# DeltaNet inverse in a hybrid decoder trunk: the first doubling on two quarters of the array, and sums of squares by a column of ones

## The chip, the core and the metric

The kernel runs on one core of one Trainium2 chip. The metric is the device time of one execution in microseconds. The core's engines work side by side: TensorE (PE, matmul; PEld is its weight load), VectorE (DVE), ScalarE (ACT), GpSimd (POOL) and SyncE (SP, which only issues loads and stores here). They wait for each other by semaphores. Matrix products go to PSUM, in banks of 128 partitions by 512 numbers of four bytes.

## The reference

A decoder trunk of two layers over 256 tokens of width 2048, batch 1. Each layer normalises its input, multiplies it by one wide input matrix, mixes the result in two ways, maps it back by one output matrix and adds a gated per-layer embedding. Half of the mixing width is a gated DeltaNet with 8 heads of 128, in chunks of tokens:

```python
q = l2_norm(to_heads(q, DN_HEADS)) * (DN_HEAD_DIM ** -0.5)
k = l2_norm(to_heads(k, DN_HEADS))
...
A = jnp.where(strict, jnp.einsum("bhncd,bhnsd->bhncs", k_beta, k) * decay, 0.0)
eye = jnp.eye(C, dtype=A.dtype)
rhs = jnp.concatenate([v * beta[..., None], k_beta * jnp.exp(G)[..., None]], axis=-1)
sol = lax.linalg.triangular_solve(A + eye, rhs, left_side=True, lower=True,
                                  unit_diagonal=True)
```

Two things matter here. `l2_norm` needs, for each token and head, the sum of the squares of q and of k. And the solve needs the inverse of a unit triangular matrix. The kernel takes chunks of 128 tokens, so it inverts a 128x128 matrix for each head and each of two chunks. The other half of the mixing width is HGRN2, which the change leaves as it is.

## The kernel before

**The big products.** All weights come through `load` as tiles of 128 x 1024 (SyncE's queue, three raw buffers). `prep` splits each into a rounded part (ScalarE, L333) and the rest (VectorE, L335). `products` makes three matmuls for each weight tile from the split weights and activations, mostly 512 columns wide. `run_step` handles one such tile: 24 matmuls for two halves of the tokens. `ahead` keeps the splits two steps and the loads four steps ahead. All these, and all other matmuls, go through `PEOrder` (L274 to L281), which keeps TensorE in the order in which the program writes them. L276 is therefore the line of every matmul and L279 that of every transpose.

**The order of the rest.** A layer runs the stages "in", "out" and "gate". While their big products run, the mixers' small work is put between them: each mixer is a set of Python generators, which `spawn` starts and `tick`, called after each big step, goes on with. A `yield n` means "go on after n steps". The n of every stop are written out by hand in `DELAY` by kind (d is DeltaNet, h is HGRN2), with exceptions by group and stop in `DELAY_AT` (L32 to L48); `wait` reads them. A generator can also wait for a flag with `after`. There are four groups g of two heads in each of two layers, so eight DeltaNet units `DN`, named dn00 to dn13 in the profile (layer, group).

**One DeltaNet unit.** `dkdq` turns k and q, runs the convolution and leaves both in `kq`, tokens along the free side, for two heads hh and two chunks t. `k_side` calls `stat(0, "ssk")`: four transposes into PSUM, then four squares on ScalarE that also add up along the row. The transposed k is used again for `ktail`. From the sums come `invn` and `b`. `q_side` forms the products of k with k and q (pg), and from them `Bt` and `QK`; it sends `Bt` through DRAM on ScalarE's queue to get the 16x16 diagonal blocks F together; then comes `stat(1, "ssq")` for q; then it inverts the diagonal blocks on VectorE (L639 to L644) and brings them back through DRAM as `Tt`.

From there the inverse doubles three times, from blocks of 16 to 32, 64 and 128 (L650 to L703). Each doubling transposes a part of `Tt` (stops t16, t32, t64), makes the product pp with `Bt`, copies it to `Pp` on ScalarE (stops p16, p32, p64), makes the product px with `Tt` and writes it into `Tt`. The first doubling does this with full 128x128 products for each of the four (hh, t) pairs i and puts the result in by a mask (L662). The second works on 32x32 blocks in two parts b = 0 and 64, with all i of one part and then all of the other (L669, L678). The third works on 64x64 blocks. `dv` waits for the inverse and finishes the unit.

**Buffers.** `tmp` takes from a ring of six tiles of 128 x 512 that all mixers share; PSUM has five banks for the mixers (`pm`) and three for the big products (`pd`).

Of the kernel before, what the change touches and what calls it, by code (L numbers as in the profile page):

```python
# [25 lines left out]
def chunk_cols(chunk):  # L26
# [6 lines left out]
    "d": {'c': 1, 'D': 4, 'k': 5, 'q': 5, 'ssq': 1, 'F': 3, 'T': 9, 't16': 2, 'p16': 2, 't32': 2, 'p32': 2, 't64': 2, 'p64': 2, 'v': 5, 'z0': 1, 'S': 1, 'w': 1, 'z1': 1, 'o': 1, 'y': 3, 'yp': 1},  # L33
# [98 lines left out]
UNITS = (1, 4, 16)  # L132


NMASK = 128 + 3 * 192


def const_arrays():
    i = np.arange(128)
    c = np.zeros((128, 4 * 128 + 256), np.float32)  # L140
    c[:, 0:128] = np.eye(128)
    c[:, 128:256] = 1.0
    c[:, 256:384] = i[:, None] > i[None, :]
    c[:, 384:512] = i[:, None] <= i[None, :]
    c[:, 512:768] = (np.arange(256) % 128 != 0)[None, :]
    s, r = i[:, None], i[None, :]
    m = np.zeros((128, NMASK), np.int32)
    m[:, 0:128] = (s // 32 == r // 32) & (s % 32 < 16) & (r % 32 >= 16)
    for n, u in enumerate(UNITS):
        o = 128 + 192 * n  # L150
# [9 lines left out]
def trunk(ctx: ExitStack, tc: tile.TileContext, xT, x, pT, W, par, fw, cst, msk, eye, out):  # L160
# [338 lines left out]
    class DN:  # L499
# [62 lines left out]
        def stat(self, w, name):  # L562

            ps = pm.tile([128, 512], F32, tag="m", name=self.n + name)
            for i in range(4):
                PE.transpose(ps[:, 128 * i:128 * i + 128], self.kq[:, i // 2, i % 2, w, :], ident)
            ss = small(name)
            for i in range(4):
                S.activation(sp.tile([128, 128], F32, tag="junk", name="junk", bufs=1), ps[:, 128 * i:128 * i + 128],
                             AF.Square, accum_out=ss[:, i:i + 1])  # L570
            return ps, ss
# [12 lines left out]
        def k_side(self):  # L584
# [3 lines left out]
            pk, ss = self.stat(0, "ssk")  # L588
            self.ktail = mix("ktail", 256, 1, n + "kt")
            V.tensor_tensor(v4(self.ktail), v4(pk)[:, 0::2], v4(self.Dt)[:, 0::2, 127:128].to_broadcast([128, 2, 128]),  # L590
# [12 lines left out]
        def q_side(self):  # L603
# [7 lines left out]
            for hh in range(2):  # L611
# [4 lines left out]
                for t in range(2):  # L616
# [14 lines left out]
                            channel_multiplier=-1)  # L631
            yield self.wait("ssq")
            pq, ss = self.stat(1, "ssq")
# [18 lines left out]
            yield self.wait("t16")  # L652
            pp = pm.tile([128, 512], F32, tag="m", name=n + "pp16")
            for i in range(4):
                PE.matmul(pp[:, 128 * i:128 * i + 128], Bt[:, i], v4(Tn)[:, i], start=True, stop=True)
            Pp = tmp(n + "P16")
            S.copy(Pp, pp)
# [4 lines left out]
            V.copy_predicated(Tt, bc1(ms[:, 0:128], 4), v4(px))  # L662
# [6 lines left out]
            for b in (0, 64):  # L669
                for i in range(4):  # L670
# [7 lines left out]
            for b in (0, 64):  # L678
                for i in range(4):
# [87 lines left out]
    class HG:  # L767
# [42 lines left out]
        def q_side(self, qr):  # L810
# [38 lines left out]
            def quad_products(u, K, Q):  # L849
                for hh in range(2):  # L850
# [6 lines left out]
                    o, mo = 0, 128 + 192 * UNITS.index(u)  # L857
# [285 lines left out]
```

## Time and profile before

| | |
|---|---|
| median of 3 runs | 1306.22 us (1305.85 to 1307.09) |
| the profiled execution's own time | 1306.57 us |
| its span, first to last instruction | 1304.9 us |
| granted TensorE clock, mean | 0.995 of full speed |
| TensorE busy (matmuls; weight loads) | 1271.2 us; 1066.3 us |
| VectorE, ScalarE, GpSimd busy | 960.6, 780.1, 105.5 us |
| matmul instructions | 6592 |

The span is that of one execution under the profiler. A busy TensorE overlaps its instructions, so the sum of lengths isn't the time that they take. A float32 product appears in the trace as two matmuls with a weight load each.

### The profile page before, as it was taken

To read this page: it belongs to the slowest core of one execution; us is meant where nothing else is said; L and a number is where in the kernel's file an instruction comes from. 1 tells how busy PE (TensorE), PEld (TensorE's weight loads), DVE (VectorE), ACT (ScalarE), POOL (GpSimd) and SP (SyncE) were. 2 spreads that over 40 slices of the span, in tenths; PEclk is the share of its full clock that TensorE was granted. 3 is DMA by queue.
4 is the path that set the end of the run, shared out by engine and by line. 5 is a ranking of instruction groups with operands and counts; after the bars stand their busy time and mean duration, and the time that the engine had idled before them with its cause. 6 is when DMAs were issued, how large, how long until landed. Compare 5 with 4: busy or idle time off the path is not lost.

```text
span 1304.9 us, 18389 instructions
## 1 busy us (share of the span) xinstructions
PE 1271.2 (97%) x6592; PEld 1066.3 (82%) x6592; DVE 960.6 (74%) x1787; ACT 780.1 (60%) x1389; POOL 105.5 (8%) x88
## 2 busy tenths in 40 slices
PE   7999999999999999999999999999999999999995
PEld 6888788888888888888888887888888888888884
DVE  5689877976798766547558897788877968565575
ACT  5766666666665654347557666667656666443464
POOL 0200010010001110000001100111100012000010
PEclk9999999999999999999999999999999999999998
DMA  9555455445554455665555554544555444555553
GB/s 321 187 172 155 146 157 167 132 150 179 156 173 154 130 174 175 192 189 185 187 170 176 153 162 154 172 144 139 161 186 174 138 162 146 187 186 183 193 193 114
DMA packets 78172, 221.01 MB, mean 169 GB/s; under 512 B 15488, under 2 KB 24576, under 8 KB 78080
## 3 DMA queue, kind: packets, MB, share of 16 engines
q1 hardware_dynamic: 59408, 212.49, 51.1%
q10 hardware_dynamic: 18672, 7.34, 2.2%
q8 instruction: 52, 0.85, 0.3%
q14 instruction: 40, 0.33, 0.1%
HBM read 215.08 MB, written 4.72 MB: 168 GB/s over the span
## 4 chain that ended last, share of the span: by engine, by line
PE 69%; DVE 18%; ACT 5%; issue 3%; DMA 3%; POOL 0%; ACTq 0%; SPq 0%; DVEq 0%
PE gate L276 13%; PE out L276 12%; DVE wlo L335 6%; PE in0hf L276 5%; PE in1dk L276 5%; PE in1hf L276 5%; PE in1dv L276 5%; PE in0dv L276 4%; PE in0hi L276 3%; PE in1hi L276 3%; PE in0dk L276 2%; DMA raw<-W 2%; ACT whi L333 2%; PE up L276 2%; PE in1dz L276 1%
## 5 line engine op out<-in xcount | busy, mean ns | idle before, releaser
L335 DVE TENSOR_TENSOR wlo<-raw,whi 128x1024 fp32r<-128x1024 f32 (+2 forms) x398 | 485.5, 1223 | 245.9 <-ACT whi L333 244.3
L333 ACT ACTIVATE whi<-raw 128x1024 fp32r<-128x1024 f32 (+2 forms) x398 | 414.6, 1044 | 342.1 <-PE out L276 84.4
L276 PE MATMUL in0dk<-whi,n0hi 128*128 128x512 f32 x128 | 51.6, 403 | 2.5 <-ACT whi L333 2.5
L276 PE MATMUL in1dk<-whi,n1hi 128*128 128x512 f32 x128 | 51.2, 400 | 2.4 <-ACT pg L981 2.4
L276 PE MATMUL in0dk<-wlo,n0hi 128*128 128x512 f32 x128 | 50.8, 397 | 1.8 <-DVE wlo L335 1.6
L276 PE MATMUL in1hf<-whi,n1hi 128*128 128x512 f32 x128 | 52.0, 406 | 0.0
L276 PE MATMUL in0hf<-whi,n0hi 128*128 128x512 f32 x128 | 52.0, 406 | 0.0
L276 PE MATMUL in0hi<-whi,n0hi 128*128 128x512 f32 x128 | 51.9, 406 | 0.0
L276 PE MATMUL in1hi<-whi,n1hi 128*128 128x512 f32 x128 | 51.9, 406 | 0.0
L276 PE MATMUL in1dk<-wlo,n1hi 128*128 128x512 f32 x128 | 50.1, 391 | 0.9 <-DVE wlo L335 0.8
L276 PE MATMUL in1hi<-wlo,n1hi 128*128 128x512 f32 x128 | 50.1, 391 | 0.5 <-DVE wlo L335 0.5
L276 PE MATMUL in0dk<-whi,n0lo 128*128 128x512 f32 x128 | 50.5, 395 | 0.0
L276 PE MATMUL gate<-whi,g0hi 128*128 128x512 f32 x128 | 50.1, 392 | 0.0
L276 PE MATMUL in0hi<-wlo,n0hi 128*128 128x512 f32 x128 | 50.0, 391 | 0.1
L276 PE MATMUL in1hf<-whi,n1lo 128*128 128x512 f32 x128 | 50.0, 391 | 0.0
L276 PE MATMUL in0hf<-whi,n0lo 128*128 128x512 f32 x128 | 50.0, 391 | 0.0
L276 PE MATMUL in1hi<-whi,n1lo 128*128 128x512 f32 x128 | 50.0, 390 | 0.0
L276 PE MATMUL in0hi<-whi,n0lo 128*128 128x512 f32 x128 | 50.0, 390 | 0.0
L276 PE MATMUL in1dk<-whi,n1lo 128*128 128x512 f32 x128 | 49.9, 390 | 0.0
L276 PE MATMUL in0hf<-wlo,n0hi 128*128 128x512 f32 x128 | 49.9, 390 | 0.0
L276 PE MATMUL in1hf<-wlo,n1hi 128*128 128x512 f32 x128 | 49.9, 390 | 0.0
L276 PE MATMUL gate<-whi,g1hi 128*128 128x512 f32 x128 | 49.9, 390 | 0.0
(1575 smaller groups left out, 3304.8 us busy)
## 6 DMA issues: line engine op xcount, KB each, us to landing
raw<-W SPq DMA_DIRECT2D x384, 512.0 KB, 3.5
raw<-W SPq DMA_DIRECT2D x8, 544.0 KB, 4.4
xt<-xT SPq DMA_DIRECT2D x4, 512.0 KB, 6.3
h<-x SPq DMA_DIRECT2D x4, 512.0 KB, 8.7
out_dram<-h SPq DMA_DIRECT2D x6, 256.0 KB, 3.1
fw<-fw ACTq DMA_DIRECT2D x2, 512.0 KB, 4.9
pin<-pT ACTq DMA_DIRECT2D x2, 256.0 KB, 3.0
out_dram<-h ACTq DMA_DIRECT2D x2, 256.0 KB, 2.8
```

The costliest lines, as they stand in the source:

```text
L276: return tc.keep_in_program_order(nc.tensor.matmul(*a, **k))
L333: S.activation(hi[:, sl], raw[:, sl], AF.Copy)
L335: V.tensor_tensor(lo[:, sl], raw[:, sl], hi[:, sl].bitcast(F32), ALU.subtract)
```

## The change

The statistic's method is replaced by two, `squares` (one square on ScalarE from `kq` into a temporary) and `sums` (four matmuls with the squares as weights and one column of ones, whose result is one column each). k keeps two of its four transposes, those that `ktail` reads, and gets one more step between the square and the sums; q keeps none, and its square is made before the stop ssq.

The first doubling works on two quarters of the array, rows and columns 0 to 63 and 64 to 127, and moves only the 16 columns of each block of 32 that can be other than zero; its copy spreads the result out again, its masked copy becomes two, and the mask shrinks from 128 to 32 columns. The second doubling gets its two loops exchanged, so that the two parts alternate. Beside that the table of delays changes.

```diff
-    "d": {'c': 1, 'D': 4, 'k': 5, 'q': 5, ...
+    "d": {'c': 1, 'D': 4, 'k': 4, 'q': 5, ...
...
-    "d0D": 5, "d0k": 6, "d0p16": 3, "d0q": 6, "d0t64": 3, "d0v": 6,
-    "d1S": 3, "d1p64": 1, "d1ssq": 3, "d1t16": 4, "d1yp": 2,
-    "d2D": 5, "d2k": 4, "d2t64": 4, "d2y": 4, "d2yp": 2, "d2z1": 2,
-    "d3k": 6, "d3o": 2, "d3p64": 3, "d3v": 6,
-    "h0K": 2, "h0a": 4, "h0u16": 3, "h0yp": 2,
-    "h1f": 2, "h1u": 3, "h1x": 3, "h1yp": 3,
+    "d0D": 5, "d0F": 2, "d0k": 7, "d0p16": 4, "d0p64": 1, "d0q": 7, "d0t16": 1, "d0yp": 3,
+    "d1D": 6, "d1S": 3, "d1p64": 1, "d1q": 4, "d1ssq": 3, "d1t16": 4, "d1y": 4, "d1yp": 2, "d1z1": 2,
+    "d2D": 5, "d2k": 5, "d2p32": 1, "d2t32": 1, "d2t64": 4, "d2y": 4, "d2yp": 2, "d2z0": 2, "d2z1": 2,
+    "d3k": 5, "d3o": 2, "d3p64": 3, "d3v": 6,
+    "h0K": 2, "h0a": 4, "h0c": 2, "h0u1": 1, "h0u16": 3, "h0yp": 2,
+    "h1f": 2, "h1u": 3, "h1yp": 3,
...
-    "h3K": 1, "h3f": 2, "h3y": 3, "h3yp": 2,
+    "h3K": 1, "h3f": 2, "h3u1": 3, "h3y": 3, "h3yp": 2,
...
-NMASK = 128 + 3 * 192
+NMASK = 32 + 3 * 192
...
-    m[:, 0:128] = (s // 32 == r // 32) & (s % 32 < 16) & (r % 32 >= 16)
+    m[:, 0:32] = (s % 64 // 32 == np.arange(32)[None, :] // 16) & (s % 32 < 16)
...
-        def stat(self, w, name):
-
-            ps = pm.tile([128, 512], F32, tag="m", name=self.n + name)
-            for i in range(4):
-                PE.transpose(ps[:, 128 * i:128 * i + 128], self.kq[:, i // 2, i % 2, w, :], ident)
-            ss = small(name)
-            for i in range(4):
-                S.activation(sp.tile([128, 128], F32, tag="junk", name="junk", bufs=1), ps[:, 128 * i:128 * i + 128],
-                             AF.Square, accum_out=ss[:, i:i + 1])
-            return ps, ss
+        def squares(self, w, name):
+            sq = tmp(self.n + name)
+            S.activation(sq, self.kq.rearrange("p h t w c -> p (h t) w c")[:, :, w, :], AF.Square)
+            return sq
+
+        def sums(self, ps, o, sq):
+
+            for i in range(4):
+                PE.matmul(ps[:, o + i:o + i + 1], sq[:, 128 * i:128 * i + 128], ones[:, 0:1], start=True, stop=True)
+            return ps[:, o:o + 4]
...
-            pk, ss = self.stat(0, "ssk")
+            sq = self.squares(0, "k2")
+            yield 1
+            pk = pm.tile([128, 512], F32, tag="m", name=n + "ssk")
+            for hh in range(2):
+                PE.transpose(pk[:, 128 * hh:128 * hh + 128], self.kq[:, hh, 0, 0, :], ident)
+            ss = self.sums(pk, 256, sq)
...
+            sq = self.squares(1, "q2")
             yield self.wait("ssq")
-            pq, ss = self.stat(1, "ssq")
+            ss = self.sums(pm.tile([128, 512], F32, tag="m", name=n + "ssq"), 0, sq)
...
             pp = pm.tile([128, 512], F32, tag="m", name=n + "pp16")
-            for i in range(4):
-                PE.matmul(pp[:, 128 * i:128 * i + 128], Bt[:, i], v4(Tn)[:, i], start=True, stop=True)
+            two = lambda ap: ap.rearrange("p (b c) -> p b c", b=2)
+            for i in range(4):
+                for b in (0, 64):
+                    PE.matmul(pp[b:b + 64, 32 * i:32 * i + 32], Bt[b:b + 64, i, b:b + 64],
+                              two(v4(Tn)[b:b + 64, i, b:b + 64])[:, :, 0:16], start=True, stop=True)
             Pp = tmp(n + "P16")
-            S.copy(Pp, pp)
+            S.copy(Pp[:, :256].rearrange("p (a w b) -> p a w b", w=2, b=16),
+                   pp[:, :128].rearrange("p (a b) -> p a b", b=16).unsqueeze(2).to_broadcast([128, 8, 2, 16]))
             yield self.wait("p16")
             px = pm.tile([128, 512], F32, tag="m", name=n + "px16")
             for i in range(4):
-                PE.matmul(px[:, 128 * i:128 * i + 128], v4(Pp)[:, i], Tt[:, i], start=True, stop=True)
-            V.copy_predicated(Tt, bc1(ms[:, 0:128], 4), v4(px))
+                for b in (0, 64):
+                    PE.matmul(px[b:b + 64, 32 * i:32 * i + 32], Pp[b:b + 64, 64 * i:64 * i + 64],
+                              two(Tt[b:b + 64, i, b:b + 64])[:, :, 16:32], start=True, stop=True)
+            for b in (0, 64):
+                V.copy_predicated(Tt[b:b + 64, :, b:b + 64].rearrange("p i (b c) -> p i b c", b=2)[:, :, :, 16:32],
+                                  bc1(ms[b:b + 64, 0:32], 4).rearrange("p i (b c) -> p i b c", b=2),
+                                  px[b:b + 64, :128].rearrange("p (i b c) -> p i b c", i=4, b=2))
...
             pp = pm.tile([128, 512], F32, tag="m", name=n + "pp32")
-            for b in (0, 64):
-                for i in range(4):
+            for i in range(4):
+                for b in (0, 64):
...
-            for b in (0, 64):
-                for i in range(4):
+            for i in range(4):
+                for b in (0, 64):
                     PE.matmul(px[b:b + 32, 32 * i:32 * i + 32], Pp[b + 32:b + 64, 32 * i:32 * i + 32],
                               Tt[b + 32:b + 64, i, b + 32:b + 64], start=True, stop=True)
```

More of the change, by code (lines that the diff above doesn't have):

```diff
@@ L32 @@
 DELAY = {
-    "d": {'c': 1, 'D': 4, 'k': 5, 'q': 5, 'ssq': 1, 'F': 3, 'T': 9, 't16': 2, 'p16': 2, 't32': 2, 'p32': 2, 't64': 2, 'p64': 2, 'v': 5, 'z0': 1, 'S': 1, 'w': 1, 'z1': 1, 'o': 1, 'y': 3, 'yp': 1},
+    "d": {'c': 1, 'D': 4, 'k': 4, 'q': 5, 'ssq': 1, 'F': 3, 'T': 9, 't16': 2, 'p16': 2, 't32': 2, 'p32': 2, 't64': 2, 'p64': 2, 'v': 5, 'z0': 1, 'S': 1, 'w': 1, 'z1': 1, 'o': 1, 'y': 3, 'yp': 1},
     "b": {'o': 1, 'g': 4},
@@ L147, in const_arrays @@
     m = np.zeros((128, NMASK), np.int32)
[L148 removed]
+    m[:, 0:32] = (s % 64 // 32 == np.arange(32)[None, :] // 16) & (s % 32 < 16)
     for n, u in enumerate(UNITS):
[L150 removed]
+        o = 32 + 192 * n
         for d in (1, 2, 3):
@@ L587, in k_side @@
             yield self.after("D")
-            pk, ss = self.stat(0, "ssk")
+            sq = self.squares(0, "k2")
[4 more added lines that the diff above has]
+            ss = self.sums(pk, 256, sq)
             self.ktail = mix("ktail", 256, 1, n + "kt")
-            V.tensor_tensor(v4(self.ktail), v4(pk)[:, 0::2], v4(self.Dt)[:, 0::2, 127:128].to_broadcast([128, 2, 128]),
+            V.tensor_tensor(v4(self.ktail), v4(pk)[:, 0:2], v4(self.Dt)[:, 0::2, 127:128].to_broadcast([128, 2, 128]),
                             ALU.mult)
@@ L856, in quad_products @@
                     Av = A[:, 2 * hh:2 * hh + 2].rearrange("p i (n x) -> p i n x", x=4 * u)
-                    o, mo = 0, 128 + 192 * UNITS.index(u)
+                    o, mo = 0, 32 + 192 * UNITS.index(u)
                     for d in (1, 2, 3):
```

## The prediction

> **What bounds the kernel now.** I read the page first: the span, the busy shares and the chain that ended last; then the busy time of one long stretch (PE first), and then what TensorE waited for (who <- whom, us in total, times, longest).
>
> ```profile
> span 1304.9 us, 18389 instructions
> PE 1271.2 (97%) x6592; PEld 1066.3 (82%) x6592; DVE 960.6 (74%) x1787; ACT 780.1 (60%) x1389; POOL 105.5 (8%) x88
> PE 69%; DVE 18%; ACT 5%; issue 3%; DMA 3%; POOL 0%; ACTq 0%; SPq 0%; DVEq 0%
> ```
> ```profile
> 50.00:1290.00 1240.00, 1231.46 (x6394) 1032.06 (x6394) 925.53 (x1707) 744.45 (x1313) 102.68 (x78) 1.00 0.53 166
> ```
> ```profile
> PE in0dz L276 <- ACT whi L333: 8.2, 1, 8.2
> PE in0dk L276 <- ACT whi L333: 2.5, 1, 2.5
> PE in1dk L276 <- ACT pg L981: 2.4, 1, 2.4
> PE in0dk L276 <- DVE wlo L335: 1.6, 2, 0.8
> ...
> PE in0dv L276 <- DVE wlo L335: 0.2, 1, 0.2
> ```
>
> TensorE is busy for 1231.46 of the 1240 us from 50 to 1290, at a granted clock of 1.00. Of its waits, 8.2 and 2.5 us lie in the first 50 us, and 2.4 us is the turn between the layers; the eleven other rows, from the 1.6 to the 0.2 shown last, add up to about 6.2 us. So the time is the sum of what TensorE has to push through, and a step costs or saves what it adds to or takes from that sum, whatever it does for ScalarE (60%) or VectorE (74%).
>
> A busy TensorE overlaps its own instructions, so I don't use durations as prices. I use the **delay of the next big matmul**: how much later the second projection matmul (512 columns, spaced 0.227 us in a stream) starts than it would with nothing between. A group's price is the distance from the last big matmul ahead of it to the second one behind it, less 2 x 0.227.
>
> **The terms on TensorE.** The fences from here on are from the timeline (start, length, what) unless said otherwise. First the four transposes of one statistic (L566), as they are now:
>
> ```profile
> 341.63 0.39 PE L276 MATMUL in0dv<-whi,n0lo 128*128 128x512 f32 x1
> 341.86 0.60 PE L279 MATMUL dn03ssq<-cs,dn03kq 128*128 128x128 f32 x4
> ...
> 342.53 0.40 PE L276 MATMUL in0hf<-wlo,n0hi 128*128 128x512 f32 x1
> ```
>
> 342.53 - 341.63 - 0.454 = 0.446 us for four passes, 0.111 each. In their place come matmuls that hold 128x128 squares as weights and move one column of ones. A matmul in float32 is two passes here, each with a weight load of its own (the two-column product pG at L534 shows as x2), so one statistic becomes 4 x 2 = 8 passes. The nearest row is pG: 128x128 weights, two columns.
>
> ```profile
> 941.10 0.61 PE L276 MATMUL dn13pD<-dn13ug,SLr 128*128 128x512 f32 x2
> 941.55 0.28 PE L276 MATMUL dn13pG<-gg,cs 128*128 128x2 f32 x2
> ...
> 942.00 0.39 PE L276 MATMUL in1dk<-wlo,n1hi 128*128 128x512 f32 x1
> ```
> ```profile
> 301.51 0.19 PEld L276 LDWEIGHTS in0dk<-whi,n0hi 128*128 128x128 f32 x1
> 301.62 0.19 PEld L276 LDWEIGHTS in0dk<-wlo,n0hi 128*128 128x128 f32 x1
> ```
>
> From the first pD to the second big matmul behind pG lie 0.90 us; three 512-column matmuls take 0.681 of it, so pG's two passes cost 0.22, or 0.11 each, though they move two columns. The second fence shows why: behind a short matmul a weight load follows the one ahead by 0.11 us, and such a stream runs at the pace of its loads. A column of ones is therefore no cheaper per pass than a 128-column transpose, and there are twice as many. q: 8 x 0.11 - 0.446 = +0.43. k keeps two transposes for ktail: 2 x 0.111 + 8 x 0.11 - 0.446 = +0.66. Per head group +1.09 us, and with 4 groups x 2 layers = 8: **+8.7 us**. The ends: if only the matmuls' own starts counted, pG's second one began about 0.03 us after its first (0.28 less its own length, 0.25 by its two-column row below), and 128 passes would cost 3.8 instead of 14.1 us: 3.8 - 48 x 0.111 = -1.5 us. For the other end, no 128-column pass here costs more than 0.111. By tile, pG's durations (min, median, max in ns):
>
> ```profile
> L276 PE MATMUL dn13pG<-gg,cs x2: 166/208/251, 941.6 to 941.6; 128*128 128x2 f32 x2
> ```
>
> The Trainium skill says the same of the load ("TensorE: Matmul & The Clock Gate", section LDWEIGHTS): its time goes by the weight columns alone, columns / 1.2 GHz, which would be an estimated 107 ns at 128, and it speaks against this edit. The Trainium skill, same page, section Back-to-back issue gap, gives about 60 cycles (25 ns) for an isolated matmul of 1 to 64 columns; by that line alone the term would fall to the lower end. The 0.11 measured on pG decides for the load.
>
> **First doubling** (pp16, px16). Now: four 128x128x128 products, 8 passes. Then: eight of 64x64 weights with 32 columns, 16 passes, alternately in two quarters that share neither rows nor columns. The rows: px16 now, and the 64x64 product of the third doubling, 8 passes in one quarter.
>
> ```profile
> 310.98 0.39 PE L276 MATMUL in0dk<-whi,n0lo 128*128 128x512 f32 x1
> 311.21 1.05 PE L276 MATMUL dn02px<-dn02Tt,dn02P 128*128 128x128 f32 x8
> ...
> 312.33 0.40 PE L276 MATMUL in0dk<-wlo,n0hi 128*128 128x512 f32 x1
> ```
> ```profile
> 238.35 0.39 PE L276 MATMUL in0dv<-whi,n0lo 128*128 128x512 f32 x1
> 238.67 0.68 PE L276 MATMUL dn01px<-dn01Tt,dn01P 64*64 64x64 f32 x8
> ...
> 239.62 0.39 PE L276 MATMUL in0dv<-wlo,n0hi 128*128 128x512 f32 x1
> ```
>
> Now 1.35 - 0.454 = 0.90 us; the 64x64 block costs 1.27 - 0.454 = 0.81, of which only about 0.46 (0.68 less a last matmul's 0.22) is its passes: the first one starts 0.32 instead of 0.227 after the big matmul, and the next big ones come late too. The new blocks pay that change of array shape, which the old ones don't. If the two quarters run side by side, 16 passes take what 8 do: 0.81, **-0.09 a block**, 16 blocks, **-1.4 us**. Half the columns bring nothing if the load sets the pace, as above. Ends: quarters one after the other, 8 passes more at 0.46/8 = 0.06: +0.37 a block, +6.0 us; passes at the 0.03 of the 32x32 blocks below: 8 x 0.03 for 0.46, so 0.59, -0.31 a block, -4.9 us. I take side by side, because the next rows show it for quarters with other rows and columns.
>
> **Second doubling, order alone** (pp32, px32). Eight matmuls of 32x32, 16 passes: today four of one part, then four of the other.
>
> ```profile
> 324.33 0.39 PE L276 MATMUL in0dv<-whi,n0lo 128*128 128x512 f32 x1
> 324.65 0.59 PE L276 MATMUL dn02px<-dn02Tt,dn02P 32*32 32x32 f32 x16
> ...
> 325.51 0.40 PE L276 MATMUL in0dv<-wlo,n0hi 128*128 128x512 f32 x1
> ```
> ```profile
> 324.65 0.31 PE L276 MATMUL dn02px<-dn02Tt,dn02P 32*32 32x32 f32 x4
> ```
> ```profile
> 324.77 0.34 PE L276 MATMUL dn02px<-dn02Tt,dn02P 32*32 32x32 f32 x9
> ```
>
> The second and third fences are the passes in flight at 324.79 and at 324.93: four, then nine. The second part joins while the first still runs, so parts do overlap, into one PSUM bank, but only near the seam. All 16 start within 0.59 - 0.19 = 0.40 us. One part's first four start within 0.31 - 0.19 = 0.12, then one per 0.03: eight in about 0.25. In turn from the start, both should fit into that: **-0.15 a block**, 16 blocks, **-2.4 us**. Ends: 0 and -2.4. The Trainium skill, "TensorEngine Tiling (Array Packing)", section Restrictions and Gotchas, says that different row tiles cannot access the same PSUM bank at once; it would put both doublings at their upper ends. Nine in flight speaks against it.
>
> **Off TensorE.**
>
> ```profile
> L569 ACT ACTIVATE junk<-dn00ssk x4: 258/277/277, 72.5 to 73.7; 128x128 f32<-128x128 f32 x4
> L657 ACT COPY dn02P<-dn02pp x1: 569/569/569, 306.2 to 306.2; 128x512 f32<-128x512 f32 x1
> L696 ACT COPY dn02P<-dn02pp x1: 367/367/367, 337.5 to 337.5; 64x256 f32<-64x256 f32 x1
> L434 ACT ACTIVATE s1sq<-h x8: 613/632/635, 597.6 to 662.6; 128x512 f32<-128x512 f32 x8
> L662 DVE COPY_PREDICATED dn02Tt<-ms,dn02px x1: 734/734/734, 312.3 to 312.3; 128x512 f32<-128x512 int32 x1
> ```
>
> ScalarE gives up four squares with read-outs per statistic (starts 72.5 to 73.7, about 1.5 us) for one 128x512 square of 0.63, and the P16 copy falls from 0.57 to about 0.37: some 1.9 us per group. The masked copy becomes two over half the rows and a quarter of the elements, each no longer than the present 0.73, on VectorE at 74%. None is on the path; cost and gain 0, hidden under TensorE's stream. ScalarE could at best take some of the 6.2 us of waits away. New waits: the sums wait for a square on ScalarE, and behind them in TensorE's order stand the projections. The cover is one step, 24 big matmuls x 0.227 = 5.4 us. If ScalarE is later than that, TensorE stands still for as long as the square's 0.63 and whatever is queued ahead of it exceed the cover. The squares also take two more turns in the ring of six temporaries, so an instruction that needs a buffer may hold up ScalarE. The moved delays shift k, q, F, t16, p16 and others by a step or two in groups 0 to 2; the last group's k with its extra step stays at 6, so nothing late in the layer moves. Their DMAs (Bt out, the diagonal in, Tt back) move along on ScalarE's queue, with the steps' slack. I take 0 for all of it, ends -6.2 (every wait gone) and +6.2 (as many again).
>
> **Sum**: 8.7 - 1.4 - 2.4 = +4.9 us. The profiled execution took 1306.57 (span 1304.9 and 1.7 around it), 0.35 above the median of 1306.22; on the median I forecast **1311.1 us**, 0.4% slower. A difference under 0.2%, 2.6 us, can hardly be told from none.
>
> **Rivals.**
> 1. *The one-column passes cost their columns, not their loads.* Place: the 16 statistics. At 0.03 a pass, -1.5 - 1.4 - 2.4 = -5.3: 1300.9, faster. Break-even: 128 p = 5.3 + 3.8, p = 0.071 us; below it the change wins. For it: pG's second matmul starts 0.03 after the first. Against: its 0.22 on the next big matmul. Chance 0.14. The 60 cycles of the Trainium skill, named above, belong to this rival.
> 2. *Waits go.* Same sum, but lighter ScalarE and new delays take away 2.5 to 6 of the 6.2 us: 1305 to 1308.6, no change that can be told. The waits are many and small, 0.8 at most, which speaks against taking most of them. Chance 0.20.
> 3. *The quarters don't overlap* (the edit doesn't do what it says): +8.7 + 6.0 + 0 = 1320.9. Against: nine in flight. Chance 0.06.
> 4. *New waits*, at the ring or at the squares, 2.5 to 6 us: 1313.6 to 1317. Chance 0.14.
> The forecast within 2.5 us, 1308.6 to 1313.6: chance 0.46. The range leaves out rivals 1 and 3, 0.20 together, and takes in 2 and 4, with the ends of the unknown waits: 1304 to 1317. Faster 0.14 (rival 1), no change 0.20 (rival 2), slower 0.46 + 0.06 + 0.14 = 0.66.
>
> **What would show it.** Each sum block of 8 passes delays the next big matmul by 0.88 us (0.21 if rival 1 is right), pp16 and px16 by 0.81 (1.27 if serial), pp32 and px32 by 0.57. TensorE's waits between 50 and 1290 us, the turn left out, should stay near 6; 2.5 more or less there makes the forecast wrong with every price right.

## The result, and the profile after

| | before | changed |
|---|---|---|
| median | 1306.03 us (1303.59 to 1307.09, 4 runs) | 1327.59 us (1326.69 to 1328.48, 4 runs) |
| the profiled execution's own time | 1306.57 us | 1326.69 us |
| its span | 1304.9 us | 1324.7 us |
| granted TensorE clock, mean | 0.995 | 0.991 |

The ratio is 1.0169 with a 95% interval of 1.0154 to 1.0184: the changed kernel is 21.6 us slower by the medians and 22.1 by the ratio (0.0169 x 1306). The forecast was 4.9 us slower, with a range that ended at 1317. The sign was right; the size was not, and the time lies outside the range.

The page of the changed kernel, the lines that answer to the three of before:

```profile
span 1324.7 us, 18687 instructions
PE 1281.1 (97%) x6800; PEld 1070.4 (81%) x6800; DVE 955.7 (72%) x1795; ACT 765.9 (58%) x1277; POOL 105.0 (8%) x88
PE 81%; DVE 10%; DMA 3%; ACT 3%; issue 1%; POOL 1%; ACTq 0%; SPq 0%; DVEq 0%
```

The shares tell little: TensorE shows 97% here as well, and 10 us more busy time. The stretch from 50 to 1290 us says more (busy time of PE, PEld, DVE, ACT and POOL, each with its count, then the granted clock, DMA share and GB/s):

```profile
50.00:1290.00 1240.00, 1218.85 (x6504) 1017.29 (x6503) 908.06 (x1700) 718.00 (x1183) 99.30 (x76) 1.00 0.51 164
```

TensorE now stands idle for 1240 - 1218.85 = 21.2 us of it; before, it was 1240 - 1231.46 = 8.5. That is 12.6 us more of waiting, the term that the prediction had set to 0. What TensorE waited for in the changed kernel (who <- whom, us in total, times, longest):

```profile
PE dn11pp L276 <- DVE dn11T L657: 3.1, 1, 3.1
PE dn01pp L276 <- DVE dn01T L657: 3.0, 1, 3.0
PE in1dk L276 <- DVE wlo L335: 2.4, 2, 1.8
...
PE dn01pg L276 <- DVE dn01kq L559: 1.8, 1, 1.8
PE dn11pg L276 <- DVE dn11kq L559: 1.8, 1, 1.8
```

Two kinds among them are new and large, each once in either layer: pp16 of group 1 waits 3 us for T, the transposed inverse that starts the first doubling, and pg of group 1 waits 1.8 us for `kq`. They make 9.7 us together; the rest are smaller waits for the split weights (wlo) and others.

**The prices, block by block.** The delay of the next big matmul, read as before (start, length, what):

```profile
269.18 0.39 PE L276 MATMUL in0dv<-whi,n0lo 128*128 128x512 f32 x1
269.41 0.95 PE L276 MATMUL dn02ssq<-cs,dn02q 128*128 128x1 f32 x8
...
270.54 0.40 PE L276 MATMUL in0hi<-wlo,n0hi 128*128 128x512 f32 x1
```
```profile
314.27 0.39 PE L276 MATMUL in0dk<-whi,n0lo 128*128 128x512 f32 x1
314.59 0.66 PE L276 MATMUL dn02pp<-dn02T,dn02Bt 64*64 64x32 f32 x16
...
315.51 0.39 PE L276 MATMUL in0dk<-wlo,n0hi 128*128 128x512 f32 x1
```
```profile
328.20 0.39 PE L276 MATMUL in0dv<-whi,n0lo 128*128 128x512 f32 x1
328.52 0.44 PE L276 MATMUL dn02px<-dn02Tt,dn02P 32*32 32x32 f32 x16
...
329.23 0.40 PE L276 MATMUL in0dv<-wlo,n0hi 128*128 128x512 f32 x1
```

Eight passes over a column of ones: 270.54 - 269.18 - 0.454 = 0.91 us (0.88 forecast). Sixteen quarter passes: 1.24 - 0.454 = 0.79 (0.81). Sixteen 32x32 passes in turn: 1.03 - 0.454 = 0.58 (0.57). With the prices of before from the prediction, and taking the eight passes of k's sums at the price of q's, q costs 0.91 - 0.446 = 0.46 and k 0.46 + 0.222 = 0.68 per head group, 8 x 1.14 = +9.1; the doublings give 16 x (0.79 - 0.90) = -1.8 and 16 x (0.58 - 0.73) = -2.4. The sum is **+4.9 us**, the very sum of the forecast.

**The account of the profiled executions.** The idle time is read from two single executions, so it is set against their own difference: 19.8 us of span. Over the whole span TensorE is idle (span less its busy time) for 43.6 us against 33.7. That is 9.9 us more, since 2.7 of the 12.6 come back at the two ends. Stretches in which TensorE's clock was at half speed, which the last section shows, cost 4.7 us more than before (an estimate: half of TensorE's busy time in them). That leaves 5.2 us for the work itself, against 4.9 of prices.

**Where the idle time begins.** VectorE at k's side of group 1 in the changed kernel (timeline; the bracket tells the idle time ahead of an instruction and what ended it):

```profile
175.44 0.42 DVE L595 TENSOR_TENSOR dn01kt<-dn01ssk,dn01Dt 128x256 f32<-128x256 f32 x1 [1.78 <-PE dn00pS L276]
...
177.24 0.15 DVE L602 TENSOR_SCALAR b<-dn01ssk 128x4 f32<-128x4 f32 x1
...
178.30 0.17 DVE L605 TENSOR_SCALAR nb<-b 128x4 f32<-128x4 f32 x1
178.51 0.61 DVE L623 SCALAR_TENSOR_TENSOR dn01Bt<-dn01pg,nb,dn01Dt 128x128 f32<-128x128 f32 x2
```

`ktail` (kt) has one buffer, so group 1's can be written only when group 0's has been read for the last time, by pS of dn00, the product of v and kt. Behind kt stand `b`, `nb` and then `Bt`, from which the whole inverse starts. The same tiles before, by tile (ns min/median/max, then first and last start), and `b` from the timeline of before:

```profile
L590 DVE TENSOR_TENSOR dn01kt<-dn01ssk,dn01Dt x1: 402/402/402, 175.0 to 175.0; 128x256 f32<-128x256 f32 x1
```
```profile
139.37 0.17 DVE L597 TENSOR_SCALAR b<-ssk 128x4 f32<-128x4 f32 x1
```
```profile
L618 DVE SCALAR_TENSOR_TENSOR dn01Bt<-dn01pg,nb,dn01Dt x4: 340/340/351, 160.9 to 162.0; 128x128 f32<-128x128 f32 x4
```

Before, kt was written as late as now, at 175.0 us, and nothing minded: `b` had been made at 139.37 and `Bt` at 160.9. There `b` reads the sums from a small tile of its own in SBUF (`b<-ssk`). The change puts k's sums into the PSUM tile that also holds the transposes for `ktail` (`ss = self.sums(pk, 256, sq)`), so kt and `b` now read one tile (`dn01ssk` in both rows), and they run in the program's order, kt first. ScalarE's logarithm of the sums, the third reader of that tile, starts at 176.0 us, also behind kt. `Bt` of dn01 comes 17.6 us later (178.51 for 160.92), and pp16, the inverse's first use, is reached by TensorE 3.0 us too early.

### The profile page after: what moved, and what is told of

Same layout as the page of the kernel before. It is cut to its first block, busy times and chain, and to the rows that moved or that the text cites. A ratio compares the mean times of both kernels' runs of the same rounds, so it can differ in the third digit from the quotient of the medians.

```text
span 1324.7 us, 18687 instructions
## 1 busy us (share of the span) xinstructions
PE 1281.1 (97%) x6800; PEld 1070.4 (81%) x6800; DVE 955.7 (72%) x1795; ACT 765.9 (58%) x1277; POOL 105.0 (8%) x88
## 4 chain that ended last, share of the span: by engine, by line
PE 81%; DVE 10%; DMA 3%; ACT 3%; issue 1%; POOL 1%; ACTq 0%; SPq 0%; DVEq 0%
PE out L276 13%; PE gate L276 13%; PE in0hi L276 6%; PE in1dk L276 5%; PE in1hi L276 5%; PE in0dv L276 5%; PE in1dv L276 5%; PE in0hf L276 5%; PE in1hf L276 4%; PE in0dk L276 4%; DVE wlo L335 3%; PE up L276 2%; ACT whi L333 1%; PE in0dz L276 1%; PE in1dz L276 1%
```

## Experiments

Theory K: `ktail`'s one buffer now holds up `Bt`, and this is the greater part of the loss. Theory D: the new table of delays costs the time by itself. Theory S: the sums cost more than 0.11 us a pass. Each difference below is the ratio to the kernel before, of the same chip, times the median of before. Executions of one kernel spread by up to some 7 us, so only the intervals decide.

**1. `ktail` with two buffers.**

```diff
-            self.ktail = mix("ktail", 256, 1, n + "kt")
+            self.ktail = mix("ktail", 256, 2, n + "kt")
```

> The changed kernel with two buffers for ktail instead of one; nothing else. Theory K (the kt chain): in the changed kernel the first reader of k's PSUM tile is the product that writes ktail, which has one buffer and so waits for the pS matmul of the group ahead; the logarithm (ScalarE) and b (VectorE) read the sums out of the same tile and are put behind it, so nb, Bt, the solve and pp16 come late. With two buffers that wait is gone: Bt of dn01 is written near 165 us instead of 179, the 3.0 us wait of pp16 in dn01 and dn11 is gone, TensorE's waits fall from 31 to 17 to 22 us in all and the time to 1312 to 1319 us. Theory D (the moved delays alone set TensorE's waits): the waits stay, 1325 to 1329 us. Theory P (the new matmuls cost more than their trace spacing shows): no change either, 1325 to 1329 us.

Measured: 1317.00 us, ratio 1.0094 (1.0077 to 1.0112), so 12.3 us slower than before and no longer 22.1. By tile, `Bt` is back where it was, and the two waits of pp16 are gone from the list of waits:

```profile
L623 DVE SCALAR_TENSOR_TENSOR dn01Bt<-dn01pg,nb,dn01Dt x4: 341/342/351, 160.5 to 161.6; 128x128 f32<-128x128 f32 x4
```
```profile
50.00:1290.00 1240.00, 1224.65 (x6547) 1022.66 (x6547) 913.43 (x1708) 725.30 (x1194) 109.69 (x78) 1.00 0.52 165
```
```profile
PE dn10pS L276 <- DVE dn11fx L650: 1.8, 1, 1.8
PE dn11pg L276 <- DVE dn11kq L559: 1.8, 1, 1.8
PE dn01pg L276 <- DVE dn01kq L559: 1.8, 1, 1.8
```

kt and `b` of dn01 in this run's timeline, both early again:

```profile
138.31 0.42 DVE L595 TENSOR_TENSOR dn01kt<-dn01ssk,dn01Dt 128x256 f32<-128x256 f32 x1
139.79 0.15 DVE L602 TENSOR_SCALAR b<-dn01ssk 128x4 f32<-128x4 f32 x1
```

One number in the code, and nearly half of the loss is gone. From 50 to 1290 us the idle time is 15.4 us, 6.8 above before. The profiled execution is the fastest of the four (1314.92 us), 8.2 us over before's by its span: 5.3 are idle time, 4.6 are left for the work (4.9 by the prices), and it saves 1.7 because it has no stretch at half clock, where before has one at 46.5 us. What is left of the waits are several of 1.8 us, those of pg among them.

**2. k's sums in a PSUM tile of their own**, `ktail` with one buffer as in the change.

```diff
-            ss = self.sums(pk, 256, sq)
+            ss = self.sums(pm.tile([128, 512], F32, tag="m", name=n + "ssk2"), 0, sq)
```

> The changed kernel with k's sums in a PSUM tile of their own instead of beside the transposes; ktail keeps its one buffer. Theory K: ktail may still wait for pS of the group ahead, but the logarithm and b no longer stand behind it, so Bt comes early again and the time falls as with two buffers, 1312 to 1319 us; one PSUM bank more is in use until b has read it, which may cost up to 2 us. Theories D and P: no change, 1325 to 1329 us.

Measured: 1320.46 us, ratio 1.0117 (1.0103 to 1.0130). `Bt` of dn01, by tile:

```profile
L623 DVE SCALAR_TENSOR_TENSOR dn01Bt<-dn01pg,nb,dn01Dt x4: 341/342/351, 164.9 to 166.0; 128x128 f32<-128x128 f32 x4
```

```profile
142.03 0.16 DVE L602 TENSOR_SCALAR b<-dn01ssk 128x4 f32<-128x4 f32 x1
177.20 0.41 DVE L595 TENSOR_TENSOR dn01kt<-dn01ssk,dn01Dt 128x256 f32<-128x256 f32 x1
```

kt is as late as ever, and `b` no longer minds. So it takes both: the buffer makes kt wait, the tile makes `b` wait for kt. Taking away either brings `Bt` forward, by 18.0 and by 13.6 us, and takes 4.6 and 5.0 us off TensorE's idle time over the whole span (43.6 us; 39.0 and 38.6 in these two). That shows theory K's chain from two sides. That it is the greater part of the loss isn't shown: two buffers take back 9.8 of the 22.1 us and the tile 6.8, and the time here lies above the 1312 to 1319 expected. The profiled execution here has five windows of 3.4 us at half clock and that of two buffers none, so the two times differ though the idle times don't.

**3. Sums alone, without the new delays or the doublings** (the kernel before with `squares` and `sums`; k's stop one step earlier, since the square takes a step), and the same with two `ktail` buffers.

```diff
-            yield self.wait("k")
+            yield self.wait("k") - 1
...
-            pk, ss = self.stat(0, "ssk")
+            sq = self.squares(0, "k2")
+            yield 1
...
+            ss = self.sums(pk, 256, sq)
```

> The kernel before with the sums by a column of ones alone; delays as before, k one step less ahead of its square so that the sums stand where the transposes stood. By spacing the sums cost 16 x 0.90 + 8 x 0.22 - 16 x 0.446 = +9.1 us on TensorE: 1315 us with waits as before. Theory K adds the kt chain, which is in this kernel too: +5 to +12 us, 1320 to 1327 us. Theory D: 1313 to 1317 us.

> The kernel before with the sums alone, as in the run of the sums (1364 us), and two buffers for ktail. Prices alone: 1315 us. In that run TensorE waited 22 us in front of yp of dn00 and dn10, for a product that stands on VectorE between the steps of the late solve of the next group, and 11.6 us in front of ssk for the square on ScalarE. Theory K: the 22 us go with the kt chain, the 11.6 us and their half-clock stretches stay: 1326 to 1338 us. If the kt chain isn't what delays the solve: over 1350 us.

Measured: 1364.17 us, ratio 1.0448 (1.0434 to 1.0463), and with two buffers 1335.50, ratio 1.0231 (1.0216 to 1.0246). The first lies 37 us above all that was expected, the second within theory K's range. With the old delays the same chain costs 28 us. It is then yp that waits longest: TensorE's transposes of a group's finished output yt, which VectorE writes only behind the late solve of the next group. With two buffers the waits for k's square take its place. From the lists of waits of the two:

```profile
PE dn10yp L279 <- DVE dn10yt L462: 11.4, 1, 11.4
PE dn00yp L279 <- DVE dn00yt L462: 10.5, 1, 10.5
```
```profile
PE dn00ssk L276 <- ACT dn00k L564: 4.1, 1, 4.1
...
PE dn10ssk L276 <- ACT dn10k L564: 2.3, 1, 2.3
...
PE dn01ssk L276 <- ACT dn01k L564: 1.4, 1, 1.4
```

The wait at the squares, a rival of the prediction, is thus real with the old delays. With the new ones, in the changed kernel, none of these rows stands in the list.

**4. The new delays alone** on the kernel before.

```diff
-    "d0D": 5, "d0k": 6, "d0p16": 3, "d0q": 6, "d0t64": 3, "d0v": 6,
+    "d0D": 5, "d0F": 2, "d0k": 7, "d0p16": 4, "d0p64": 1, "d0q": 7, "d0t16": 1, "d0yp": 3,
...
```

> The kernel before with the delays of the change alone, no other edit. Theory D (the moved delays by themselves make the loss): 1316 to 1328 us. Theory K (the loss comes from k's sums and the ktail buffer; the new delays only soften it): 1306 to 1314 us, no wait of pp16 for the transposed T16, Bt of dn01 near 162 us.

Measured: 1335.92 us, ratio 1.0241 (1.0226 to 1.0255), above both ranges. This doesn't convict the table: its k stops reckon with the step between square and sums, which the old code lacks, so by the code k's side comes a step too early for q's half of `kq` (pg of dn03 and dn13 waits 4.3 us each). Old code with the new table costs 31 us, the new sums with the old table 58, both changes together 22. Table and edits belong together, and neither can be judged without the other; theory D as a cost by itself stays undecided.

**5. Sixty-four columns of ones in place of one**, to price a pass (the same sums stand in every column, and one is read).

```diff
-                PE.matmul(ps[:, o + i:o + i + 1], sq[:, 128 * i:128 * i + 128], ones[:, 0:1], start=True, stop=True)
-            return ps[:, o:o + 4]
+                PE.matmul(ps[:, o + 64 * i:o + 64 * i + 64], sq[:, 128 * i:128 * i + 128], ones[:, 0:64], start=True, stop=True)
+            return ps[:, o:o + 256:64]
```

> The changed kernel with 64 columns of ones moved in place of one (the result is read from one column of each 64; the sums are the same). Load theory (a pass with 128x128 weights goes at 0.11 us because of its weight load): each block of 8 passes still delays the next big matmul by 0.90 us, and TensorE's prices stay. Column theory: 128 passes x 63 columns x about 0.8 ns = +6.7 us, 1334 us. Clock theory (the granted clock halves where TensorE waits or moves little, and the sums of one column count as little work): fewer or shorter half-clock stretches beside the sums, 1322 to 1327 us; if only the waits count, 1326 to 1329 us.

Measured: 1326.31 us, ratio 1.0159 (1.0143 to 1.0175), which cannot be told from the changed kernel's 1.0169. The block of eight passes of q's sums delays the next big matmul by 0.90 us, as with one column (0.91). Sixty-four times the columns cost nothing, which fits a pass that costs its weight load. Theory S and the prediction's rival 1 fall.

**6. The doublings alone** (both, all groups, old delays and old statistics), and the second doubling's order alone.

```diff
             for i in range(4):
                 for b in (0, 64):
-            for b in (0, 64):
-                for i in range(4):
...
```

> The kernel before with the two doublings of the change alone (quarters for pp16 and px16, parts in turn for pp32 and px32, the small mask); statistics and delays as before. By the trace of the changed kernel a quarter block delays the next big matmul by 0.787 instead of 0.895 us and a 32x32 block by 0.571 instead of 0.717: 16 x (-0.108 - 0.146) = -4.1 us, so 1302 us with waits as before, 1300 to 1304. Theory P, under which the small matmuls cost more than their spacing shows: 1306 or more.

> The kernel before with one edit, the two loops of pp32 and px32 exchanged, so that the two parts alternate. Price theory: 16 blocks from 0.717 to 0.571 us, -2.3 us, and next to nothing else moves, so 1303 to 1304 us. Order theory (any edit shifts how the small work falls on VectorE and ScalarE, and waits of a few us come or go with it): the blocks have their new price, but the time lies anywhere from 1302 to 1308 us, and the difference is found in waits or half-clock stretches.

Measured: 1306.14 us, ratio 1.0002 (0.9993 to 1.0011); the order alone 1304.55, ratio 0.9995 (0.9986 to 1.0004). Neither can be told from before, though the blocks' prices promise -4.2 and -2.4 us. By its time alone the first would bear out theory P. The account of its profiled execution doesn't: its span is 0.9 us shorter than before's, with 2.1 us more idle time and 1.7 more lost to half clock, so the work itself is 4.7 us shorter. TensorE's list of waits tells where the saving went:

```profile
PE dn10px L276 <- ACT dn10P L661: 1.9, 1, 1.9
PE dn00px L276 <- ACT dn00P L661: 1.9, 1, 1.9
```

The products of group 0's first doubling are done sooner, but the copy of pp16 to P16 on ScalarE stands behind other work there and doesn't come sooner; px16 waits for it, and TensorE stands with it.

**7. Another stop for group 0**: px16 a step later (p16 from 3 to 4), and with T a step earlier to make up for it (t16 from 2 to 1 as well).

```diff
-    "d0D": 5, "d0k": 6, "d0p16": 3, ...
+    "d0D": 5, "d0k": 6, "d0p16": 4, ...
```

> The doublings alone with group 0's stop p16 at 4 instead of 3 and t16 left at 2, so px16 of group 0 comes one step later than in the doublings' run and the rest of its inverse as well. In the run with t16 at 1 and p16 at 4 the wait for P16 went and 3.0 us in front of pg of group 1 came. Price theory: no wait for P16, no new wait, 1301 to 1303 us. Order theory: another wait of some us appears, 1304 to 1310 us.

> The doublings alone, as in the run of the doublings, with group 0's stop p16 at 4 instead of 3 and its t16 at 1 instead of 2, so that the same number of steps is used. In that run px16 of group 0 waited 1.9 us for the copy of P16 in both layers, and a half-clock stretch of 3.4 us began at each of the two waits. If these two things ate the 4.1 us that the blocks save: no such wait, no such stretch, 1301 to 1303 us. If the saving of the blocks isn't real in a stream: 1305 to 1307 us.

Measured: 1308.74 us, ratio 1.0033 (1.0020 to 1.0046), and 1309.51, ratio 1.0028 (1.0018 to 1.0037). No gain from either; the first is what its order theory expected, the second lies above both of its ranges. The wait for P16 went and others came: pg of dn01 and dn11 for `kq`, 1.8 us each in the one and 3.0 in the other. The changed table has p16 of group 0 at 4 too, and pg of group 1 waits above 1 us in no run that has it at 3.

**8. The doublings with q's sums alone**, k's statistic as before.

> The doublings and the sums by a column of ones for q alone; k keeps its transposes and squares on the row, delays as before. q's sums have a PSUM tile of their own, without ktail. By prices -4.1 + 8 x 0.46 = -0.4 us, and the waits and half-clock stretches of the doublings' run on top (+4): 1306 to 1311 us. Theory K says that k's half alone makes the large loss, so nothing near the 1364 us of both sums. If the square ahead of the sums is what stalls TensorE, q shows it as well: over 1315 us.

Measured: 1308.28 us, ratio 1.0022 (1.0012 to 1.0032), 2.9 us over before and 2.6 over the doublings alone; the price of q's sums is 8 x 0.46 = 3.7. q's half of the change costs no more than its price: its sums have a PSUM tile for themselves and no `ktail`.

**9. What is left once `ktail` has two buffers**: q of group 1 back to 5 steps, then to 6, since pg waits for q's half of `kq`.

```diff
-    "d1D": 6, "d1S": 3, "d1p64": 1, "d1q": 4, ...
+    "d1D": 6, "d1S": 3, "d1p64": 1, "d1q": 6, ...
...
-            self.ktail = mix("ktail", 256, 1, n + "kt")
+            self.ktail = mix("ktail", 256, 2, n + "kt")
```

> The changed kernel with two buffers for ktail and group 1's delay q back from 4 to 5, so that pg no longer follows k's sums in the same step. With two buffers alone 1.8 us of waits for the q half of kq remain in front of pg in dn01 and dn11. If those two waits and what they trigger are the next part of the loss: they vanish, and the time falls by 3 to 5 us from the 1317.0 of two buffers, to 1312 to 1314 us. If the other small waits grow in their place: 1315 to 1318 us.

> The changed kernel with two ktail buffers, and q of group 1 put off by two steps (delay 4 to 6), so that q's half of kq no longer falls into the steps of k's sums. Theory W (after two ktail buffers, the next part of the loss are the waits of dn01pg and dn11pg for q's half of kq, 1.8 us each, and the half-clock stretches that begin at them): both waits go, 1312 to 1315 us. Rival C (the rest is the prices of 5.1 us and half-clock stretches that begin anywhere): 1315 to 1318 us, as the two ktail buffers alone had. Rival M (q late by two steps makes yt or the second statistic late): waits for dn01ssq or yt of 1.5 us and more appear in place of pg's, 1317 or above.

Measured: 1317.00 us, ratio 1.0088 (1.0074 to 1.0102), with pg's waits unchanged, since at 5 steps q still falls into the step of k's sums and the run told nothing apart; at 6 steps 1332.56, ratio 1.0198 (1.0176 to 1.0220). There pg waits no more, and the list has in its place:

```profile
PE dn01px L276 <- ACT dn01P L712: 8.2, 1, 8.2
PE dn11px L276 <- ACT dn11P L712: 8.2, 1, 8.2
```

With all of group 1's inverse later, the third doubling's copy of P falls on ScalarE behind the whole convolution of group 2. A wait of 1.8 us was exchanged for one of 8.2. The time is rival M's, but M looked for the new wait at ssq or yt; it came at px of the third doubling.

**10. The doublings without group 0's wait.** Three ways: the quarters in groups 1 to 3 alone, with group 0 on its full products and the new order of the 32x32 products everywhere; and the doublings everywhere with the copy of P16 on VectorE, in group 0 or in all.

```diff
+            if self.g == 0:
+                for i in range(4):
+                    PE.matmul(pp[:, 128 * i:128 * i + 128], Bt[:, i], v4(Tn)[:, i], start=True, stop=True)
...
+            else:
```
```diff
-            S.copy(Pp[:, :256].rearrange("p (a w b) -> p a w b", w=2, b=16),
+            (V.tensor_copy if self.g == 0 else S.copy)(Pp[:, :256].rearrange("p (a w b) -> p a w b", w=2, b=16),
```

> The kernel before with the new order of the 32x32 products in all groups and the two quarters for pp16 and px16 in groups 1, 2 and 3 alone; group 0 keeps its full 128x128 products, so its px16 comes later behind pp16 than a quarter's would. Theory P (the doublings' own 4 us are real, and group 0's px16, which stood 1.9 us waiting for P16 in both layers and began a half-clock stretch there, gave them back): no wait above 1 us at px16 in group 0, 1301 to 1303.5 us. Rival C (the gain is lost wherever the quarters are, since the clock's half-speed stretches come anyway): 1304.5 to 1307, the same as before.

> The doublings alone (both parts, all groups), with group 0's copy of P16 on VectorE in place of ScalarE, where it stood behind two other instructions. Theory P (the copy's place in ScalarE's order is what px16 of group 0 waited for): px16's two waits of 1.9 us fall below 0.6, no half-clock stretch begins there, 1301 to 1304 us. Rival V (VectorE, at some 73%, has the copy no earlier: the wait stays above 1.2 us): 1305 to 1307.

> The doublings alone, with the copy of P16 on VectorE in all groups. Theory P: as with group 0 alone, since the other groups' copies were not waited for, 1301 to 1304 us. Rival V (VectorE's added 8 copies, some 0.3 to 0.4 us each, delay the solve and the statistics that TensorE waits for): waits for VectorE grow by 1 us or more, 1305 to 1309.

Measured: the quarters in groups 1 to 3 **1301.05 us, ratio 0.9957 (0.9940 to 0.9974)**, 5.6 us faster than before (3.4 to 7.8). With the copy on VectorE 1304.42, ratio 0.9986 (0.9974 to 0.9998), in group 0, and 1303.38, ratio 0.9977 (0.9966 to 0.9988), in all. Rows from the lists of waits of the first and the second, and from the second's timeline of VectorE:

```profile
PE dn00px L277 <- ACT dn00P L659: 0.6, 1, 0.6
```
```profile
PE dn10px L276 <- issue: 1.5, 1, 1.5
PE dn00px L276 <- issue: 1.5, 1, 1.5
```
```profile
131.75 0.42 DVE L661 COPY dn00P<-dn00pp 128x256 f32<-128x256 f32 x1
```

On VectorE too the copy stands behind other work and ends at 132.2 us, where px16 starts; the list names no releaser for its 1.5 us of wait in each layer ("issue"). With group 0's copy alone the rival's condition came true, and neither its time of 1305 to 1307 nor theory P's of 1301 to 1304 did. Eight copies more on VectorE cost nothing that shows. Leaving group 0 as it was keeps its wait at the 0.6 us of before, and the other groups' gains are kept. This version beats both kernels. Its price sum is -2.4 - 12 x 0.11 = -3.7 us, within the interval.

## Why the prediction missed

**TensorE is the bound, and the time is a sum of its blocks' delays**: right. The measured prices add up to +4.9, as forecast.

**Statistics +8.7**: right (+9.1), and the reason with it as far as tested: 64 columns cost what one does.

**First doubling -1.4, second -2.4**: right as prices (-1.8 and -2.4). That quarters and 32x32 parts run side by side into one PSUM bank is shown by 0.79 us for 16 passes, where the third doubling's 8 took 0.81. The Trainium skill ("TensorEngine Tiling (Array Packing)", section Restrictions and Gotchas) says that different row tiles cannot access the same PSUM bank simultaneously, which would have put them one after the other; the trace disagrees. But a price is a gain only if what TensorE does next is ready, and in group 0 it was not (experiments 6 and 10).

**The step that failed** is the one on what lies off TensorE: "I take 0 for all of it, ends -6.2 (every wait gone) and +6.2 (as many again)". Idle time from 50 to 1290 us rose by 12.6 us, twice the upper end. The prediction had named this as its own sign of being wrong: 2.5 us more there, with every price right. Its rival 4, new waits, had the kind right, but at half the size and in the wrong places: it named the squares and the ring of temporaries. The largest waits came from a buffer that the diff doesn't touch: `ktail`'s one, which had been written late before, off the path, and got onto the path because the sums moved into the tile that it reads. The row for it was in the trace of before: dn01kt at 175.0 us, 35.6 us behind `b` at 139.37, though the program writes it ahead of `b`. An instruction that runs so far behind its place in the program is waiting for something; the question to ask was who will now stand behind it.

"The moved delays shift k, q, F, t16, p16 and others by a step or two" failed with it: `Bt` of dn01 moved by 17.6 us, more than three steps of 5.4, and with the same stops and two buffers it is back at 160.5 us.

The sum also had no term for TensorE's clock: a wait counted as its own length. The half-clock stretches beside the new waits cost 4.7 us more than before.

**The size of the step.** The same account for the runs that part the change, each profiled execution less that of before, in us. The work is what is left of the span without idle time and half clock; the prices are sums of the blocks' delays.

| run | span | idle time | half clock | work | prices |
|---|---|---|---|---|---|
| changed | 19.8 | 9.9 | 4.7 | 5.2 | 4.9 |
| two `ktail` buffers (1) | 8.2 | 5.3 | -1.7 | 4.6 | 4.9 |
| sums in a tile of their own (2) | 15.9 | 4.9 | 6.4 | 4.6 | 4.9 |
| sums alone (3) | 58.8 | 34.3 | 15.6 | 8.9 | 9.1 |
| sums, two buffers (3) | 28.2 | 7.1 | 12.4 | 8.7 | 9.1 |
| delays alone (4) | 32.0 | 20.9 | 10.9 | 0.2 | 0 |
| doublings alone (6) | -0.9 | 2.1 | 1.7 | -4.7 | -4.2 |
| order alone (6) | -4.7 | -1.0 | -1.7 | -2.0 | -2.4 |
| quarters in groups 1 to 3 (10) | -4.7 | -2.6 | 1.7 | -3.8 | -3.7 |

In these rows the work is the prices to 0.5 us; in six of the other eight runs to 1.5, in two not (-2.7 for -0.5 in experiment 8, and 1.9 for 4.9 with q at 6 in experiment 9). So the prices were right, and the loss beyond them is idle time and half clock.

Of the 22.1 us, two `ktail` buffers take away 9.8 (12.3 instead of 22.1 over before); 5.8 of them are idle time (21.2 to 15.4 us), and for the rest the trace offers TensorE's clock, below. What stays is 6.8 us of idle time over before, in waits of 1.8 us and less. Whether those could be had back was tried once (experiment 9), and the cure cost more; so for these the trace names the waits, but no run removed them at a profit.

**What stays open.** The order of the 32x32 products alone gave 0.7 us (interval from a gain of 1.8 to a loss of 0.5) where its price says 2.4, without a new wait above 0.6 us in its trace. That trace is of the fastest of its executions (1301.91 us), and there the price shows; what the others lost it to isn't on record. With group 0's copy on VectorE the profiled execution accounts for 2.2 us of gain (work -4.7, idle time 0.8, half clock 1.7), near the 1.8 measured; why the copies in all groups gained 3.0 isn't settled, since the trace kept is of the slowest of its executions. Which stop makes pg of group 1 wait in the changed kernel wasn't tried there; experiment 7 points at p16 of group 0.

## What to carry to other kernels

Before moving a result into a tile that something else reads, look at when that other reader runs: here sharing a tile put the two in the program's order, and a reader that waited for a buffer of its own then held up all that followed. On an engine that is 97% busy, the price of a block is right only as long as the next block's input is ready; cutting a producer short gains nothing where the copy behind it stands in another engine's queue, so make the cut in those groups alone where it is ready. A table of delays and the code that it was made for are one thing: the table alone cost 31 us and the sums without it 58, both together 22.

## What the runs showed of the hardware

TensorE's clock fell to half for 3.4 us, or a multiple of it, beside waits as short as 1.8 us. The changed kernel, in stretches (columns as for 50 to 1290 us; the clock is the number behind POOL's), then the same place before:

```profile
136.90:140.30 3.40, 2.53 (x6) 2.11 (x7) 3.27 (x8) 0.63 (x1) 0.00 (x0) 0.50 0.78 246
140.30:143.70 3.40, 3.40 (x9) 2.65 (x9) 1.21 (x4) 0.63 (x1) 0.00 (x0) 0.50 0.62 217
860.50:863.90 3.40, 3.40 (x27) 3.14 (x24) 3.01 (x5) 1.57 (x3) 0.00 (x0) 0.50 0.28 59
```
```profile
136.90:143.70 6.80, 6.80 (x45) 5.46 (x44) 5.19 (x14) 4.84 (x16) 0.00 (x0) 1.00 0.66 196
```

The first of them begins within pg's wait (pg starts at 137.77 after 1.76 us of nothing). Big matmuls in it follow each other by 0.43 us, and by 0.23 once it is over:

```profile
137.77 3.75 PE L276 MATMUL dn01pg<-dn01kq 128*128 128x256 f32 x8 [1.76 <-DVE dn01kq L559]
...
142.17 0.63 PE L276 MATMUL in0dv<-whi,n0lo 128*128 128x512 f32 x1
142.60 0.63 PE L276 MATMUL in0dv<-whi,n0hi 128*128 128x512 f32 x1
...
144.04 0.39 PE L276 MATMUL in0dv<-wlo,n0hi 128*128 128x512 f32 x1
144.27 0.39 PE L276 MATMUL in0dv<-whi,n0lo 128*128 128x512 f32 x1
```

The changed kernel spends 10.2 us in these stretches, where before had none beyond 50 us; TensorE is busy for 9.33 us of them, so at half speed they cost an estimated 4.7 us. (The profile with two `ktail` buffers has none there.) The doublings alone (experiment 6) show the same right behind both of px16's waits:

```profile
133.10:136.50 3.40, 3.40 (x10) 2.75 (x9) 3.29 (x12) 1.33 (x3) 0.00 (x0) 0.50 0.49 154
774.80:778.20 3.40, 3.40 (x10) 2.61 (x9) 3.25 (x11) 1.04 (x2) 0.00 (x0) 0.51 0.51 159
```

The Trainium skill ("TensorE: Matmul & The Clock Gate", Part 1) describes a gate with two ratios, 4/8 and 8/8, decided in free-running windows of about 3.4 us; the 0.50 and the 3.40 agree. So do the starts: 136.90 and 860.50 lie 723.6 us apart, 212 windows of 3.413 us, and 133.10 and 774.80 lie 641.7 apart, 188 of them. On this grid the same wait can have two prices. In the changed kernel pp16 of group 1 waits 2.97 us in the first layer, up to 210.17, and 3.06 in the second, up to 860.29. The second wait lies whole in the window from 857.1 to 860.5, in which TensorE is busy for 0.34 us, and a stretch at half clock follows; the first is divided between the two windows that meet at 208.56, and none follows. How busy a window must be isn't shown: one with 2.54 us of 3.41 busy stands ahead of the stretch at 136.90, and the one from 208.56 with 1.80 is followed by none.

Nor is every wait followed by such a stretch from one execution to the next: the mean clock of the two-buffer kernel's four executions was 0.990 in one, at 1321.74 us, and 0.995 to 0.996 in the others, at 1314.92 to 1317.09. So a new wait of 2 us may cost 1.7 us more than its length, or 3.4 where two stretches follow, as at pg's here. Part of the spread between executions of one kernel goes with this clock: among 23 of the kernel before on one chip the three fastest (1303.38 to 1303.74 us) had a mean clock of 0.996 to 0.997, the three slowest (1308.38 to 1309.87) 0.992 to 0.993.
